# A decoder layer's feed-forward part: three quarters of it dealt out in six eighths, with up products between the two column pairs of each down product

## The chip, the cores and the metric

The kernel runs on one core of a Trainium2 chip. TensorE (PE in the profile, its weight loads PEld) multiplies matrices, VectorE (DVE) and ScalarE (ACT) work on elements, GpSimd (POOL) and SyncE (SP) here mostly start transfers. The metric is the time of one execution in microseconds (us), the median of three runs.

## The reference

A decoder layer for 256 tokens of width 2048, in float32. A first part mixes tokens (attention and a convolution). The second part is a feed-forward layer with a hidden width of 8192:

```
u = rms_norm(h, pre_ff_gain)                      # 256 x 2048
f = square(relu(u @ w_ff1)) @ w_ff2               # 2048 -> 8192 -> 2048
h = h + rms_norm(f, post_ff_gain)
```

The change concerns this part alone. `u @ w_ff1` is called the up product here, the product with `w_ff2` the down product.

## The kernel before

**Numbers.** Each float32 operand of a product is split into a rounded part (hi) and the rest (lo), and a product is three matmuls: hi by hi, hi by lo, lo by hi. A weight chunk of 128 x 2048 (1 MB) is loaded by SP into one of three `raw` buffers (L134), cast to `wh` by ACT (L140) and its rest put into `wl` by DVE (L146). There are three pairs of `wh` and `wl` (`WBUFS`). `take` gives the next prepared chunk, `done` gives one back and prepares the next (`fill`), so that splitting runs up to three chunks ahead in the order of the list `slots`.

**The stream.** The feed-forward part begins with `stream` (L325): `h_sb` is transposed on PE (L332), scaled into the activation tiles `act` (L244, L245), and the first pair of up products is multiplied as the tiles arrive (L259, L262), the second chunk of the pair four tiles (`LAG`) behind the first. Meanwhile `square` (L702) sums up squares for the norm. Behind it the norm's factor is worked out (reduce L734, square root L314, reciprocal L315), laid on a diagonal `dg` (L738) and spread over all partitions by two small matmuls (L739) to `r2b`, which scales every up product.

**Up products.** `ws_pair` (L266) multiplies two weight chunks, one column block each: 16 matmuls of 512 columns (L271: hi and lo of `u` together, by `wh`), then 16 of 256 (L275: `wl`). The result, two blocks of 128 hidden channels, lies in one PSUM tile. `ws_sum` copies one half (L283, ACT), adds the other (L284, DVE, into `z`); then come the product with `r2b` (L893) and the squared ReLU (L896, into `sc`). An even-numbered group of four hidden blocks is laid down by `put_fast` as the seven combinations that a fast unit wants (L765 to L769, `gs`), others by `put_pair` as plain hi and lo (L240, L241, `g`).

**Down products.** The hidden width is worked in four quarters of 16 blocks. In a quarter, all eight up pairs come first, then `fast_pair` for two column pairs m of the output (1024 columns each). A `fast_pair` has four chunks of hidden channels kc, in the order 0, 2, 1, 3. For kc 0 and 1 a *fast unit* does seven products where eight would be plain (Strassen's way), from four weight parts that `fast_part` (L165) makes out of two raw chunks by sums (L162), casts (L156) and subtracts (L157): 42 matmuls (L797, L798, L800). For kc 2 and 3 two plain chunks (one for each 512 columns) do 24 matmuls each (L827 to L829). The products A1 to A7 stand in the order A1, A2, A7, A3, A5, A6, A4. After the second fast unit `combine` puts the products together (one ACT copy L804, four DVE operations L806 to L809) in `ev`; after the last plain chunk of each column block ACT copies the sum to `tmp` (L862). `ev` and `tmp` are added to the total `acc` in SBUF by accumulating transfers that POOL starts (L816, L863). The last `fast_pair` (`closing`) is arranged otherwise, and is the end of the program.

**PSUM.** In this part there are four tiles of two banks, handed out in turn by `new_ps`: an up pair takes one, a `fast_pair` all four (pa to pd); pd is the tile of the last up pair before it, and A3 is its first user.

**What sets the order.** A scheduler orders each engine's instructions by priority. Instructions wrapped in `pin` (`keep_in_program_order`) keep the order in which they are written; those of the stream and of `fast_pair` on PE are, those of `ws_pair` (without `pinned`) are not.

Of the kernel before, what the change touches and what calls it, by code (L numbers as in the profile page):

```python
# [18 lines left out]
P = 128  # L19
S = 256  # L20
# [17 lines left out]
NQ = 4  # L38
# [8 lines left out]
FAST = 2  # L47
FF_ORDER = (0, 2, 1, 3)
# [7 lines left out]
def tile_layer(ctx, tc, x, x_t, pre, vecs, lams, rope_t, subln, b_conv, post_mix, post_ff,  # L56
# [12 lines left out]
    def ff_chunks(q, m):  # L69
        if q == NQ - 1 and m == 1:  # L70
            return [(0, 0), (0, 1), (2, 0), (1, 0), (1, 1), (3, 0), (2, 1), (3, 1)]
        return [(kc, i) for kc in FF_ORDER for i in range(2)]
# [11 lines left out]
    for q in range(NQ):  # L84
        order += [w_f1[q * KT + ct] for ct in range(KT)]
        for m in range(NB // 2):
            order += [w_f2[2 * m + i, q * 4 + kc] for kc, i in ff_chunks(q, m)]
    slots, at = [], 0
    slots += [("chunk", i) for i in range(n_mix)]
    at = n_mix  # L90
    for q in range(NQ):
        slots += [("chunk", at + i) for i in range(KT)]
        at += KT
        for m in range(NB // 2):
            for kc, i in ff_chunks(q, m):
                if kc >= FAST:
                    slots.append(("chunk", at))
                elif i == 0:
                    slots += [(part, at) for part in range(4)]
                at += 1  # L100
# [647 lines left out]
    gsp = ctx.enter_context(tc.tile_pool(name="gsp", bufs=2 * FAST))  # L748
    gpool = ctx.enter_context(tc.tile_pool(name="gpool", bufs=KT // 2 - 2 * FAST))
# [7 lines left out]
    class Mixed(Act):  # L757
        def __init__(self):
            self.tiles = [None] * (KT // 2)
            self.pool, self.name = gpool, "g"  # L760
            self.s = {}
# [11 lines left out]
    def fast_pair(ga, q, m):  # L773
# [4 lines left out]
        closing = q == NQ - 1 and m == 1  # L778
        ev = None if q == 0 else evp.tile([P, NT, 2, 512], F32, name="ev")
        chunks = ff_chunks(q, m)  # L780
        plains = [c for c in chunks if c[0] >= FAST]
# [4 lines left out]
        def part(t, i):  # L786
            return total(t, i) if q == 0 else ev[:, t, i]

        def fast_unit(kc, last):
            for pair in ((A1, A2), (A7, A3), (A5, A6), (A4,)):  # L790
                wh, wl = take()
                for half, a in enumerate(pair):
                    ps = own[a] if a in own else shared[a]
                    for i in range(2):
                        g = ga.s[2 * kc + i]
                        sl = slice(half * 1024 + i * 512, half * 1024 + (i + 1) * 512)
                        pin(nc.tensor.matmul(ps, g[:, 0, a], wh[:, sl], start=(kc == 0 and i == 0), stop=False))  # L797
                        pin(nc.tensor.matmul(ps, g[:, 0, a], wl[:, sl], start=False, stop=False))  # L798
                        ends = last and i == 1 and a in own
# [3 lines left out]
        def combine():  # L803
# [6 lines left out]
            for t in range(NT if q else 0):  # L810
                span = acc[:, t, m * 1024:(m + 1) * 1024]
                half = ev[:, t].rearrange("p i n -> p (i n)")
                if closing:
                    nc.vector.tensor_tensor(span, span, half, op=ALU.add)
                else:
                    nc.gpsimd.dma_start(span, half, accum_op=ALU.add)  # L816
# [21 lines left out]
        for kc, i in chunks:  # L838
            if kc < FAST:
                if i == 0:  # L840
                    fast_unit(kc, kc == FAST - 1)
                    if kc == FAST - 1:
                        combine()
                continue
            if closing and i == 1:
# [5 lines left out]
            if closing and kc == FAST:  # L851
# [5 lines left out]
            if closing:  # L857
# [6 lines left out]
        if closing:  # L864
            plain[0, 1] = new_ps()[:, 0]
            wts = [take(), take()]
            for t in (1, 0):
                for j in range(2):
                    plain_chunk(FAST + j, 1, wts[j], t)
# [17 lines left out]
    for q in range(NQ):  # L887
        ga = Mixed()
        for j in range(KT // 2):
            ps = ws_pair(u2) if q or j else lead_ps  # L890
            z = fin2.tile([P, 2, S], F32, name="z")
            ws_sum(z, ps)
            nc.vector.tensor_tensor(z, z, r2b.unsqueeze(1).to_broadcast([P, 2, S]), op=ALU.mult)  # L893
            sc = fin2.tile([P, 8, P], F32, name="sc", bufs=1)
            gg = sc[:, 0:4].rearrange("p (a t) n -> p a (t n)", a=2)
            nc.vector.scalar_tensor_tensor(gg, z, 0.0, z, op0=ALU.max, op1=ALU.mult)  # L896
            if j < 2 * FAST:
# [86 lines left out]
```

## Time and profile before

| | us |
|---|---|
| median of three runs (1539.47, 1541.21, 1539.69) | 1539.69 |
| the profiled execution's own time | 1541.23 |
| its span | 1539.4 |
| PE busy | 1523.0 (99%) |
| DVE busy | 1274.0 (83%) |
| ACT busy | 786.3 (51%) |
| stream | about 832 to 853 |
| feed-forward part behind it | 853 to 1540 |

The busy times are those of the one profiled execution. A matmul counts as busy from its issue to its end, and neighbours overlap; how many can be issued in a time is read from the starts of neighbouring rows. An idle gap of PE in a part where PE is always busy lengthens the span by itself; idle time of other engines need not.

### The profile page before, as it was taken

Reading aid. Unit: us, or ns where it says so; the run is one execution under the profiler, and the core shown is the slowest. Engines: PE = TensorE matmul, PEld = TensorE weight load, DVE = VectorE, ACT = ScalarE, POOL = GpSimd, SP = SyncE. Lnnn points to the kernel's source line nnn. Section 1 sums busy time; section 2 is a strip of 40 time slices with the busy share of each in tenths; the row PEclk is TensorE's granted clock in tenths of the full one; section 3 lists DMA queues with packets and bytes.
Section 4 is the critical chain, followed back from the end, with each engine's and each line's share of the span. In section 5 each row is a group of like instructions: output and inputs, shape, how many; then the busy total and the mean of one; then the engine's idle time right before and its main releaser. Section 6 shows DMA issues by size and latency. Waiting matters only on the chain.

```text
span 1539.4 us, 19437 instructions
## 1 busy us (share of the span) xinstructions
PE 1523.0 (99%) x7734; PEld 1295.4 (84%) x7734; DVE 1274.0 (83%) x1605; ACT 786.3 (51%) x851; POOL 41.8 (3%) x73
## 2 busy tenths in 40 slices
PE   9999999999999999999999999999999999999997
PEld 7888888888888888888887888888888888888885
DVE  7999999999999997966546888867887778867888
ACT  7444454646554545743435645544455445644454
POOL 0000000000000000000000000000010000110010
PEclk9999999999999999999999999999999999999999
DMA  8655555454445565575554744785478755895673
GB/s 294 225 190 192 192 192 185 171 174 175 174 167 186 192 203 194 181 279 185 189 191 157 267 166 183 226 264 185 170 223 271 228 180 184 246 293 191 233 231 125
DMA packets 51484, 313.66 MB, mean 204 GB/s; under 512 B 5825, under 2 KB 5953, under 8 KB 16705
## 3 DMA queue, kind: packets, MB, share of 16 engines
q1 hardware_dynamic: 43920, 289.61, 52.6%
q0 software_dynamic: 7040, 22.02, 6.1%
q8 instruction: 60, 0.98, 0.2%
q10 hardware_dynamic: 432, 0.79, 0.2%
q14 instruction: 32, 0.25, 0.0%
HBM read 295.62 MB, written 4.19 MB: 195 GB/s over the span
## 4 chain that ended last, share of the span: by engine, by line
PE 92%; DVE 4%; ACT 2%; DMA 1%; issue 1%; SPq 0%; DVEq 0%; ACTq 0%
PE ps L271 29%; PE ps L275 15%; PE ps L292 9%; PE ps L293 9%; PE ps L294 9%; PE ps L828 4%; PE ps L829 4%; PE ps L827 3%; DVE wl L146 2%; ACT wh L140 2%; PE ps L797 2%; PE ps L798 2%; PE ps L800 2%; DMA raw<-in_w_cv_dram 1%; PE po L564 1%
## 5 line engine op out<-in xcount | busy, mean ns | idle before, releaser
L140 ACT CAST wh<-raw 128x2048 fp32r<-128x2048 f32 (+2 forms) x260 | 460.7, 1778 | 495.0 <-PE ps L294 162.6
L146 DVE TENSOR_TENSOR wl<-raw,wh 128x2048 fp32r<-128x2048 f32 (+2 forms) x260 | 551.5, 2125 | 192.5 <-ACT wh L140 188.0
L271 PE MATMUL ps<-act,wh 128*128 128x512 f32 x1984 | 479.1, 392 | 0.3 <-ACT wh L140 0.3
L271 PEld LDWEIGHTS ps<-act,wh 128*128 128x128 f32 x1984 | 364.6, 188 | 70.8 <-ACT wh L140 0.6
L275 PEld LDWEIGHTS ps<-act,wl 128*128 128x128 f32 x1984 | 256.5, 191 | 10.0
L275 PE MATMUL ps<-act,wl 128*128 128x256 f32 x1984 | 264.0, 284 | 0.0
L293 PE MATMUL ps<-wl,act 128*128 128x512 f32 x624 | 243.9, 391 | 0.0
L292 PE MATMUL ps<-wh,act 128*128 128x512 f32 x624 | 243.7, 391 | 0.0
L294 PE MATMUL ps<-wh,act 128*128 128x512 f32 x624 | 243.6, 390 | 0.0
L478 DVE SCALAR_TENSOR_TENSOR y_all<-c,vec,y_all 128x256 f32<-128x256 f32 x480 | 209.9, 478 | 0.0
L294 PEld LDWEIGHTS ps<-wh,act 128*128 128x128 f32 x624 | 117.2, 188 | 24.2
L292 PEld LDWEIGHTS ps<-wh,act 128*128 128x128 f32 x624 | 117.1, 188 | 24.1
L293 PEld LDWEIGHTS ps<-wl,act 128*128 128x128 f32 x624 | 117.2, 188 | 23.9
L156 ACT CAST wh<-raw 128x1024 fp32r<-128x1024 f32 x64 | 65.3, 1050 | 91.1 <-PE ps L829 23.4
L828 PE MATMUL ps<-wl,g 128*128 128x512 f32 x256 | 101.6, 397 | 2.2 <-DVE wl L146 1.2
L829 PE MATMUL ps<-wh,g 128*128 128x512 f32 x256 | 99.7, 390 | 0.0
L827 PE MATMUL ps<-wh,g 128*128 128x512 f32 x256 | 99.7, 390 | 0.0
L798 PE MATMUL ps<-wl,gs 128*128 128x512 f32 x224 | 87.4, 390 | 0.5 <-DVE wl L157 0.5
L797 PE MATMUL ps<-wh,gs 128*128 128x512 f32 x224 | 87.2, 389 | 0.0
L800 PE MATMUL ps<-wh,gs 128*128 128x512 f32 x224 | 87.2, 389 | 0.0
L157 DVE TENSOR_TENSOR wl<-raw,wh 128x1024 fp32r<-128x1024 f32 x64 | 76.3, 1218 | 2.0 <-PE ps L275 1.1
L156 ACT CAST wh<-sum 128x1024 fp32r<-128x1024 f32 x48 | 49.0, 1051 | 37.0 <-PE ps L271 14.3
(200 smaller groups left out, 1253.1 us busy)
## 6 DMA issues: line engine op xcount, KB each, us to landing
raw<-in_w_f_dram SPq DMA_DIRECT2D x124, 1024.0 KB, 5.0
raw<-in_w_q_dram SPq DMA_DIRECT2D x16, 1024.0 KB, 4.9
raw<-in_w_k_dram SPq DMA_DIRECT2D x16, 1024.0 KB, 4.9
raw<-in_w_v_dram SPq DMA_DIRECT2D x16, 1024.0 KB, 4.8
raw<-in_w_ga_dram SPq DMA_DIRECT2D x16, 1024.0 KB, 4.8
raw<-in_w_gc_dram SPq DMA_DIRECT2D x16, 1024.0 KB, 4.9
raw<-in_w_co_dram SPq DMA_DIRECT2D x16, 1024.0 KB, 4.8
raw<-in_w_o_dram SPq DMA_DIRECT2D x16, 1024.0 KB, 4.9
```

Of the source, the lines that this page charges most:

```text
L140: i = nc.scalar.copy(wh[:, a:b], raw[:, a:b])
L146: i = (eng or nc.vector).tensor_sub(wl[:, a:b], raw[:, a:b], wh[:, a:b].bitcast(F32))
L271: a = nc.tensor.matmul(ps[:, j], wh[:, k * P:(k + 1) * P], acts.both(k), start=(k == 0), stop=False)
L275: a = nc.tensor.matmul(ps[:, j, S:], wl[:, k * P:(k + 1) * P], acts.hi(k), start=False, stop=(k == KT - 1))
L292: nc.tensor.matmul(ps, acts.hi(k, a, b), wh[:, sl], start=(k == 0), stop=False)
L293: nc.tensor.matmul(ps, acts.hi(k, a, b), wl[:, sl], start=False, stop=False)
L294: nc.tensor.matmul(ps, acts.lo(k, a, b), wh[:, sl], start=False, stop=(k == KT - 1))
L478: i = nc.vector.scalar_tensor_tensor(y, c[:, j:j + S], vcol(ct, V_DW + j), y, op0=ALU.mult, op1=ALU.add)
L798: pin(nc.tensor.matmul(ps, g[:, 0, a], wl[:, sl], start=False, stop=False))
L827: pin(nc.tensor.matmul(ps, ga.hi(k, a, b), wh[:, sl], start=first, stop=False))
L828: pin(nc.tensor.matmul(ps, ga.hi(k, a, b), wl[:, sl], start=False, stop=False))
L829: pin(nc.tensor.matmul(ps, ga.lo(k, a, b), wh[:, sl], start=False, stop=last))
```

## The change

The first three quarters become six eighths. A list `plan` is written out: four up pairs; then for each eighth e the down product of column pair 0, two up pairs of the next eighth, the down product of column pair 1, two more up pairs; the last quarter stays whole. Each of the six eighths has one fast unit (even kc) and two plain chunks (odd kc) for a column pair. So there are 14 calls of `down` for eight of `fast_pair`, and a combine and two `tmp` sums in each but the last. The weights' list and `slots` follow the plan. The up products are pinned now. Line numbers move by 8 at first and by 9 near the end: L271 becomes L279, L284 L292, L739 L747, L797 L806, L893 L902.

```diff
-FAST = 2
-FF_ORDER = (0, 2, 1, 3)
+GROUPS = ((0, 1), (2, 3), (4, 5), (6, 7), (8, 9), (10, 11), (12, 13, 14, 15))
...
-    def ff_chunks(q, m):
-        if q == NQ - 1 and m == 1:
-            return [(0, 0), (0, 1), (2, 0), (1, 0), (1, 1), (3, 0), (2, 1), (3, 1)]
-        return [(kc, i) for kc in FF_ORDER for i in range(2)]
+    def ff_chunks(e, m):
+        out = [(kc, i) for kc in GROUPS[e] for i in range(2)]
+        if closing(e, m):
+            a, b, c, d = GROUPS[e]
+            out = [(a, 0), (a, 1), (b, 0), (c, 0), (c, 1), (d, 0), (b, 1), (d, 1)]
+        return out
+
+    def is_fast(kc):
+        return kc % 2 == 0
+
+    def closing(e, m):
+        return e == len(GROUPS) - 1 and m == 1
+
+    plan = [("up", j) for j in range(4)]
+    for e in range(len(GROUPS) - 1):
+        ups = [("up", j) for j in range(4 * e + 4, 4 * e + 8)]
+        plan += [("down", (e, 0))] + ups[:2] + [("down", (e, 1))] + ups[2:]
+    e = len(GROUPS) - 1
+    plan += [("up", j) for j in range(4 * e + 4, 4 * e + 8)] + [("down", (e, 0)), ("down", (e, 1))]
 
     order = []
     for ct in range(KT):
@@ -81,23 +94,18 @@
     for w in (w_ga, w_gc, w_co, w_o):
         order += [w[n, kc] for n in range(NB) for kc in range(4)]
     n_mix = len(order)
-    for q in range(NQ):
-        order += [w_f1[q * KT + ct] for ct in range(KT)]
-        for m in range(NB // 2):
-            order += [w_f2[2 * m + i, q * 4 + kc] for kc, i in ff_chunks(q, m)]
-    slots, at = [], 0
-    slots += [("chunk", i) for i in range(n_mix)]
-    at = n_mix
-    for q in range(NQ):
-        slots += [("chunk", at + i) for i in range(KT)]
-        at += KT
-        for m in range(NB // 2):
-            for kc, i in ff_chunks(q, m):
-                if kc >= FAST:
-                    slots.append(("chunk", at))
-                elif i == 0:
-                    slots += [(part, at) for part in range(4)]
-                at += 1
+    slots = [("chunk", i) for i in range(n_mix)]
+    for what, which in plan:
+        if what == "up":
+            slots += [("chunk", len(order) + i) for i in range(2)]
+            order += [w_f1[2 * which + i] for i in range(2)]
+            continue
+        for kc, i in ff_chunks(*which):
+            if not is_fast(kc):
+                slots.append(("chunk", len(order)))
+            elif i == 0:
+                slots += [(part, len(order)) for part in range(4)]
+            order.append(w_f2[2 * which[1] + i, kc])
...
-    def fast_pair(ga, q, m):
+    def down(ga, e, m):
...
-        closing = q == NQ - 1 and m == 1
-        ev = None if q == 0 else evp.tile([P, NT, 2, 512], F32, name="ev")
-        chunks = ff_chunks(q, m)
-        plains = [c for c in chunks if c[0] >= FAST]
+        close = closing(e, m)
+        ev = None if e == 0 else evp.tile([P, NT, 2, 512], F32, name="ev")
+        chunks = ff_chunks(e, m)
+        plains = [c for c in chunks if not is_fast(c[0])]
+        fasts = [kc for kc, i in chunks if is_fast(kc) and i == 0]
...
-            return total(t, i) if q == 0 else ev[:, t, i]
-
-        def fast_unit(kc, last):
+            return total(t, i) if e == 0 else ev[:, t, i]
+
+        def fast_unit(kc):
...
-                        pin(nc.tensor.matmul(ps, g[:, 0, a], wh[:, sl], start=(kc == 0 and i == 0), stop=False))
+                        pin(nc.tensor.matmul(ps, g[:, 0, a], wh[:, sl], start=(kc == fasts[0] and i == 0), stop=False))
                         pin(nc.tensor.matmul(ps, g[:, 0, a], wl[:, sl], start=False, stop=False))
-                        ends = last and i == 1 and a in own
+                        ends = kc == fasts[-1] and i == 1 and a in own
                         pin(nc.tensor.matmul(ps, g[:, 1, a], wh[:, sl], start=False, stop=ends))
...
-    for q in range(NQ):
-        ga = Mixed()
-        for j in range(KT // 2):
-            ps = ws_pair(u2) if q or j else lead_ps
-            z = fin2.tile([P, 2, S], F32, name="z")
-            ws_sum(z, ps)
-            nc.vector.tensor_tensor(z, z, r2b.unsqueeze(1).to_broadcast([P, 2, S]), op=ALU.mult)
-            sc = fin2.tile([P, 8, P], F32, name="sc", bufs=1)
-            gg = sc[:, 0:4].rearrange("p (a t) n -> p a (t n)", a=2)
-            nc.vector.scalar_tensor_tensor(gg, z, 0.0, z, op0=ALU.max, op1=ALU.mult)
-            if j < 2 * FAST:
-                ga.put_fast(j, sc)
-            else:
-                ga.put_pair(j, gg)
-        if q == NQ - 1:
+    ga = Mixed()
+
+    def up(j):
+        ps = ws_pair(u2, pinned=True) if j else lead_ps
+        z = fin2.tile([P, 2, S], F32, name="z")
+        ws_sum(z, ps)
+        nc.vector.tensor_tensor(z, z, r2b.unsqueeze(1).to_broadcast([P, 2, S]), op=ALU.mult)
+        sc = fin2.tile([P, 8, P], F32, name="sc", bufs=1)
+        gg = sc[:, 0:4].rearrange("p (a t) n -> p a (t n)", a=2)
+        nc.vector.scalar_tensor_tensor(gg, z, 0.0, z, op0=ALU.max, op1=ALU.mult)
+        if is_fast(j // 2):
+            ga.put_fast(j, sc)
+        else:
+            ga.put_pair(j, gg)
+
+    for what, which in plan:
+        if what == "up":
+            up(which)
+            continue
+        e, m = which
+        if (e, m) == (len(GROUPS) - 1, 0):
...
-        for m in range(NB // 2):
-            fast_pair(ga, q, m)
+        down(ga, e, m)
```

Three places show how the order moves. First TensorE at the end of the stream: `dg` is the norm's factor on a diagonal, L259/L262 and L267/L270 are the stream's own matmuls. Before:

```order
L259 MATMUL ps<-act,wh 128x512
L262 MATMUL ps<-act,wl 128x256
L271 MATMUL ps<-act,wh 128x512
L275 MATMUL ps<-act,wl 128x256 x10
L739 MATMUL aux<-dg,ones 128x128 x2
L275 MATMUL ps<-act,wl 128x256 x6
L271 MATMUL ps<-act,wh 128x512 x16
```
After:

```order
L267 MATMUL ps<-act,wh 128x512
L270 MATMUL ps<-act,wl 128x256
L747 MATMUL aux<-dg,ones 128x128 x2
L279 MATMUL ps<-act,wh 128x512 x16
L283 MATMUL ps<-act,wl 128x256 x16
```

The 16 wide matmuls of the next up pair's first chunk (L271) no longer stand between the stream's; they stand behind the broadcast of `dg`, which has moved from between the narrow ones to directly behind the stream.

Second, VectorE behind the stream, from the reduction of the sums of squares (`hss`) to the first whole weight chunk. Before:

```order
L734 TENSOR_REDUCE r_6953<-hss 128x2
L315 RECIPROCAL r_6953<-r_6953 128x2
L738 TENSOR_SCALAR dg<-ident,r_6953 128x128 x2
L146 TENSOR_TENSOR wl<-raw,wh 128x512 x4
L146 TENSOR_TENSOR wl<-raw,wh 128x2048
```
After:

```order
L742 TENSOR_REDUCE r_6953<-hss 128x2
L154 TENSOR_TENSOR wl<-raw,wh 128x512 x4
L323 RECIPROCAL r_6953<-r_6953 128x2
L746 TENSOR_SCALAR dg<-ident,r_6953 128x128 x2
L154 TENSOR_TENSOR wl<-raw,wh 128x2048
```

The four subtracts of the third weight chunk's quarters have moved ahead of the reciprocal and of `dg`.

Third, VectorE ahead of a fast unit, from the first sum of its two raw chunks to the add into `z` of the last up pair (L284, now L292); `g`, `sc` belong to the up pairs, `sum` and the 128x1024 `wl` to the fast unit. Before, second quarter, first column pair:

```order
L162 TENSOR_TENSOR sum<-raw 128x1024
L162 TENSOR_TENSOR raw<-raw 128x2x512
L157 TENSOR_TENSOR wl<-raw,wh 128x1024 x2
L162 TENSOR_TENSOR sum<-raw 128x1024
L284 TENSOR_TENSOR z<-z,ps 128x512
L162 TENSOR_TENSOR sum<-sum,raw 128x1024
L893 TENSOR_TENSOR z<-z,r2b 128x512
L157 TENSOR_TENSOR wl<-raw,wh 128x1024 x2
L896 SCALAR_TENSOR_TENSOR sc<-z 128x512
L157 TENSOR_TENSOR wl<-sum,wh 128x1024 x2
L241 TENSOR_TENSOR g<-sc,g 128x2x256
L284 TENSOR_TENSOR z<-z,ps 128x512
```
After, second eighth, second column pair (two subtracts of 128x1024, the fast unit's first part, stand directly ahead of it):

```order
L170 TENSOR_TENSOR sum<-raw 128x1024
L292 TENSOR_TENSOR z<-z,ps 128x512
L170 TENSOR_TENSOR raw<-raw 128x2x512
L902 TENSOR_TENSOR z<-z,r2b 128x512
L165 TENSOR_TENSOR wl<-raw,wh 128x1024
L170 TENSOR_TENSOR sum<-raw 128x1024
L905 SCALAR_TENSOR_TENSOR sc<-z 128x512
L165 TENSOR_TENSOR wl<-raw,wh 128x1024
L170 TENSOR_TENSOR sum<-sum,raw 128x1024
L773 TENSOR_TENSOR sc<-sc 128x256
L165 TENSOR_TENSOR wl<-sum,wh 128x1024 x2
L292 TENSOR_TENSOR z<-z,ps 128x512
```

The two sums from raw stood ahead of the first part's subtracts (L157) and now stand behind them, mixed with the work on `z`; the add into `z` of the last up pair is still behind the third part's subtracts.

## Rows read from the trace of the kernel before

**Rows 1.** Page, part 1: engine, busy us (share of span), instructions

```profile
PE 1523.0 (99%) x7734; PEld 1295.4 (84%) x7734; DVE 1274.0 (83%) x1605; ACT 786.3 (51%) x851; POOL 41.8 (3%) x73
```

**Rows 2.** Windows: bounds and length, busy us of each engine, granted clock, DMA, GB/s

```profile
830.00:833.00 3.00, 1.48 (x8) 0.65 (x7) 2.45 (x7) 1.46 (x4) 0.00 (x0) 1.00 0.72 300
835.00:838.30 3.30, 3.30 (x13) 2.73 (x13) 2.30 (x6) 2.25 (x7) 0.00 (x0) 0.51 0.00 0
832.30:850.60 18.30, 17.65 (x94) 14.82 (x94) 13.31 (x27) 14.10 (x36) 1.06 (x2) 0.91 0.32 118
853.33:1530.00 676.67, 673.94 (x3413) 571.03 (x3411) 547.28 (x498) 348.86 (x321) 35.97 (x43) 1.00 0.64 214
```

**Rows 3.** Timeline of PE: start, us, line, operation, tiles, count

```profile
1094.63 3.82 PE L271 MATMUL ps<-act,wh 128*128 128x512 f32 x16
...
1100.20 0.40 PE L797 MATMUL ps<-wh,gs 128*128 128x512 f32 x1
...
1104.31 0.39 PE L797 MATMUL ps<-wh,gs 128*128 128x512 f32 x1
...
1109.74 0.39 PE L827 MATMUL ps<-wh,g 128*128 128x512 f32 x1
1110.20 0.50 PE L828 MATMUL ps<-wl,g 128*128 128x512 f32 x1
1110.54 0.39 PE L829 MATMUL ps<-wh,g 128*128 128x512 f32 x1
```

**Rows 4.** Waits of PE: waiting line, releaser, us in all, times, longest

```profile
PEld ps L828 <- DVE wl L146: 8.9, 16, 1.6
```

**Rows 5.** Timelines of DVE and ACT beside the same fast unit

```profile
1100.47 2.36 DVE L157 TENSOR_TENSOR wl<-sum,wh 128x1024 fp32r<-128x1024 f32 x2 [2.43 <-PE ps L275]
1102.74 0.69 DVE L241 TENSOR_TENSOR g<-sc,g 128x512 fp32r<-128x512 f32 x1
1103.35 0.68 DVE L284 TENSOR_TENSOR z<-z,ps 128x512 f32<-128x512 f32 x1
...
1103.20 1.05 ACT L156 CAST wh<-sum 128x1024 fp32r<-128x1024 f32 x1 [1.66 <-PE ps L800]
...
1107.85 2.29 DVE L146 TENSOR_TENSOR wl<-raw,wh 128x2048 fp32r<-128x2048 f32 x1 [1.36 <-ACT wh L140]
```

**Rows 6.** Timeline of PE: a long fast unit, its first instruction and the one behind it

```profile
1162.52 0.39 PE L797 MATMUL ps<-wh,gs 128*128 128x512 f32 x1
...
1172.23 0.39 PE L827 MATMUL ps<-wh,g 128*128 128x512 f32 x1
```

**Rows 7.** Groups by form, 870 to 1540: busy us, mean ns, idle before

```profile
L162 DVE TENSOR_TENSOR sum<-raw 128x1024 f32<-128x1024 f32 x32 | 39.0, 1220 | 7.0 <-DMA raw<-in_w_f_dram 6.8
...
L806 DVE TENSOR_TENSOR z<-ev,ps 128x512 f32<-128x512 f32 x6 | 4.1, 679 | 0.0
```

**Rows 8.** Timeline of PE: the end of the stream

```profile
853.09 0.40 PE L271 MATMUL ps<-act,wh 128*128 128x512 f32 x1
853.33 1.35 PE L275 MATMUL ps<-act,wl 128*128 128x256 f32 x10
...
855.68 0.64 PE L271 MATMUL ps<-act,wh 128*128 128x512 f32 x2
```

**Rows 9.** Timelines of ACT and DVE behind the stream: root, dg, casts

```profile
850.66 0.30 ACT L314 ACTIVATE r<-r,epsn 128x2 f32<-128x2 f32 x1 [0.23 <-DVE r L734]
...
851.19 0.48 DVE L738 TENSOR_SCALAR dg<-ident,r 128x128 f32<-128x128 f32 x2
...
851.40 2.19 ACT L140 CAST wh<-raw 128x512 fp32r<-128x512 f32 x4 [0.44 <-PE ps L259]
```

**Rows 10.** Raw loads: the page's median to landing, and one load behind a burst

```profile
raw<-in_w_f_dram SPq DMA_DIRECT2D x124, 1024.0 KB, 5.0
...
L134 SPq DMA_DIRECT2D raw<-in_w_f_dram x1: 327/327/327, 1188.0 to 1188.0; - x1
...
DMA to landing us min/median/max: 9.2/9.2/9.2
```

More of the change, by code (lines that the diff above doesn't have):

```diff
@@ L36 @@
 NEG_INF = -1e30
-NQ = 4
 WBUFS = 3
@@ L747, in tile_layer @@
     sump = ctx.enter_context(tc.tile_pool(name="sump", bufs=3))
-    gsp = ctx.enter_context(tc.tile_pool(name="gsp", bufs=2 * FAST))
-    gpool = ctx.enter_context(tc.tile_pool(name="gpool", bufs=KT // 2 - 2 * FAST))
+    gsp = ctx.enter_context(tc.tile_pool(name="gsp", bufs=4))
+    gpool = ctx.enter_context(tc.tile_pool(name="gpool", bufs=4))
     evp = ctx.enter_context(tc.tile_pool(name="evp", bufs=1))
@@ L758, in __init__ @@
         def __init__(self):
-            self.tiles = [None] * (KT // 2)
+            self.tiles = [None] * (DFF // S)
             self.pool, self.name = gpool, "g"
@@ L809, in combine @@
             nc.vector.tensor_tensor(part(0, 1), own[A5], part(0, 0), op=ALU.subtract)
-            for t in range(NT if q else 0):
+            for t in range(NT if e else 0):
                 span = acc[:, t, m * 1024:(m + 1) * 1024]
                 half = ev[:, t].rearrange("p i n -> p (i n)")
-                if closing:
+                if close:
                     nc.vector.tensor_tensor(span, span, half, op=ALU.add)
@@ L838, in fast_pair @@
         for kc, i in chunks:
-            if kc < FAST:
+            if is_fast(kc):
                 if i == 0:
-                    fast_unit(kc, kc == FAST - 1)
-                    if kc == FAST - 1:
+                    fast_unit(kc)
+                    if kc == fasts[-1]:
                         combine()
                 continue
-            if closing and i == 1:
+            if close and i == 1:
                 continue
@@ L850, in fast_pair @@
             done()
-            if closing and kc == FAST:
+            if close and (kc, i) == plains[0]:
                 for n in range(2):
@@ L856, in fast_pair @@
                 continue
-            if closing:
+            if close:
                 first_half()
@@ L863, in fast_pair @@
                     nc.gpsimd.dma_start(total(t, i), tmp[:, t], accum_op=ALU.add)
-        if closing:
+        if close:
             plain[0, 1] = new_ps()[:, 0]
@@ L868, in fast_pair @@
                 for j in range(2):
-                    plain_chunk(FAST + j, 1, wts[j], t)
+                    plain_chunk(plains[-2 + j][0], 1, wts[j], t)
                 with tc.high_priority(offset=CHAIN):
```

## The prediction

> **What bounds the kernel now.** I read the page's busy shares first, then a table of windows, then TensorE's own sequence. PE is busy 99% of the span, DVE 83%, ACT 51% [rows 1]. The windows show that the feed-forward part (853.33 to 1530.00) is fuller still: PE 673.94 of 676.67 us, DVE 547.28, ACT 348.86, at full clock [rows 2]. So there the time is the number of TensorE instructions times their issue spacing, and whatever PE waits comes on top. In a steady stretch matmuls of 512 columns start 0.227 us apart: the 18 from 1100.20 to 1104.31 take 4.11 us, and the fast unit (42 matmuls) 9.54, from 1100.20 to 1109.74 [rows 3]. A weight chunk of the up products (16 of 512 columns, 16 of 256) takes 1100.20 - 1094.63 = 5.57. A plain chunk is 24 matmuls, 5.44.
>
> Only two kinds of PE wait recur. The first plain chunk behind a fast unit loses 0.35 us at its second instruction: 1109.74 to 1110.54 holds two spacings (0.45) and takes 0.80 [rows 3]. The waits put it down to DVE's wl, 16 times [rows 4]. The reason can be read on DVE: that chunk's subtract (2.29 us, at 1107.85) waits 1.36 for its cast [rows 5], the cast for the wh slot that the first part of the fast unit's four frees; cast and subtract take longer than the matmuls still ahead of them. The second kind is a late fast part: the unit begun at 1162.52 took 9.71, to 1172.23, 0.2 more than its 42 spacings [rows 6]. On that point the Trainium skill ("Perfetto Trace Analysis", section "Identifying the Most-Contended Engine") says matmul busy time is a poor measure of headroom and the busy share of weight loads a better one. Its measure gives 571.03 of 676.67, 84%, some headroom in which a small wait could be caught up, and the waits below would cost nothing; the constant 0.227 leaves none, and I go by the measurement.
>
> **The change part by part.**
> The matmuls of the feed-forward part are the same in kind and number: sixteen fast units, sixteen pairs of plain chunks, 64 up chunks. On TensorE that is 0. There are fourteen downs for eight, so six more combines: 24 DVE instructions of 0.679 [rows 7], 16.3 us, and 30 more ACT copies; DVE goes to (547.28 + 16.3) / 676.67 = 83% of the part. The 36 added accumulating transfers occupy POOL's queue, which waits for nothing urgent. What hides all this is that PE is the bound, so averaged it costs 0; what counts is where DVE comes late.
>
> *Start of the part.* The up products are now pinned to program order. Before, the scheduler put the 16 wide matmuls of the next pair's first chunk between the transposes and matmuls of the stream (the last at 853.09), so behind it only the 16 narrow ones remained; they end at 855.68 [rows 8]. Now the 16 wide ones stand behind the stream, and L747, the broadcast of dg, stands in front of them on PE's queue. Whoever is queued behind L747 waits for it: all of PE. Two lists changed with it: on DVE the four subtracts of 128x512 precede the reciprocal, and on ACT the four casts (2.19 us) precede the square root. Before, the root came at 850.66 and dg was begun at 851.19, ahead of the casts at 851.40 [rows 9].
> The sum, in before's time axis: the stream loses 16 x 0.227 = 3.63 us of PE work, but the other chain in it, ACT's, was busy 14.10 of 18.30 us [rows 2], so that its 4.2 us of idle time are the most that can go. Sixteen hand-overs from PE to ACT and back keep part of these: I put the most at 3.0, the least at 1.1, and take 2.0, near the middle. The stream then ends at 853.3 - 2.0 = 851.3. The casts wait for the last wide matmul on the stream's first chunk, four pairs of 0.35 before the end, so they run 850.0 to 852.2; root to first L747 is 0.8 (0.53 to dg, a dg of 0.24), so 853.0; the first L279 at 853.3; the chunk ends 5.57 later at 858.9. Against 855.68 that is **+3.2 us**. By the two ends of the shrinking it is +2.2 or +4.1.
>
> *The wait in front of A3.* The fourth product group of a fast unit in order of execution (A3 in the code) begins 18 matmuls in, at 1104.31, and writes the PSUM tile that the last up pair used, so it waits for DVE's add into z. Before, this add ran from 1103.35 for 0.68 [rows 5], to 1104.03: 0.28 early. Counted from the unit's start the add may begin at +3.4. Now it depends on what DVE has to do from the moment that the unit's two raw chunks are there and first needed, 8.6 us ahead of the unit (two chunks of 5.57 minus the two subtracts, 1.14 apart by 1100.47 to 1102.74 [rows 5], begun 0.27 after a slot is freed). For the downs (e,1) with e from 1 the list shown above then runs: sum, z add (0.6), sum of two raws, the cast of it (1.05 [rows 5], the z product inside it), subtract, sum, 0.6, subtract, sum, 0.33, two subtracts. That is eight DVE steps of 1.14 (the sums cost as much, 1.22 each with their overlap [rows 7]), 1.53 of short ones and the cast: 9.12 + 1.53 + 1.05 = 11.7, so the z add starts at +3.1 to +3.25, and there is nothing to spare. For the downs (e,0) with e from 2 a subtract of g (0.61) stands in it instead of the 0.33 one: +3.4 to +3.5, a loss of 0.1. For the first three and the last, DVE does the two sums before the subtracts, as before, and nothing is lost.
> So the loss is set by when the raw chunks land. A load lands after 5.0 us in the median, but the one issued at 1188.0 took 9.2 [rows 10], behind the accumulating transfers of the down that ended at 1172.23 + 11.3 = 1183.5 [rows 6]. It stands where a fast unit's second raw will now stand, four up chunks (22.3 us) ahead of 1205.8: it lands at 1197.2, exactly the 8.6 ahead. Before, a quarter's first fast unit came 16 up chunks (89 us) behind such a burst; now eleven come four behind one. With raws on time the nine places lose 4 x 0.1, 0.4 in all; with each 0.35 late, 5 x 0.23 + 4 x 0.48 = 3.1. I take the middle, **+1.7**, since the one load seen there is exactly on the edge. Ends: 0 and 5 (each late by 0.55).
>
> *Small.* The slip in the unit at 1162.52, the fourth of four downs in a row, I read as a raw load late behind a burst; that place no longer exists: -0.2. The 16 losses of 0.35 stay, because slots and casts per fast unit are the same: 0.
>
> The sum is 3.2 + 1.7 - 0.2 = **+4.7 us**. The profiled execution took 1541.23 (span 1539.4 and 1.8 around it), so 1545.9 in its terms; it was 1.54 above the median of 1539.69, against which the forecast is **1544.4**. About 0.2%, 3.1 us, can be told from no change; the bound lies at 1542.8.
>
> **The rivals.**
> 1. *Only the start costs* (A3's wait is covered, as DVE gains time from the thinner stretches): for it speaks that my walk misses the edge by a tenth; against it the 9.2 us landing. 3.2 - 0.2: 1542.7.
> 2. *The stream shrinks fully.* If PE's order alone set the stream (it was busy 17.65 of 18.30 us there [rows 2]), all 3.63 come off: 5.2 - 3.6 = +1.6, less 0.2, A3 covered: 1541.1.
> 3. *The other side: the 0.35 losses go.* One mechanism: with up products spread out, DVE and ACT have earlier free time, the first plain chunk's split is done before the fast unit ends, 16 x 0.35 = 5.6 gained, against 3.2 lost: 1537.3. It decides once the split can start 0.35 earlier. Against it: cast and subtract wait for a slot that the same PE instruction frees, not for a busy engine; for it, nothing in the rows.
> 4. *Raws come late for all eleven fast units behind a burst*, a microsecond each instead of a few tenths: 1539.7 + 3.0 + 11 = 1554, at half of it 1549.
> 5. *DVE becomes the bound* in the stretches of one down and two ups: all 16.3 us show, 1556. Against it 83%.
> 6. *The clock.* Before, PE did 1.48 us of work in 830 to 833 and the granted clock then stood at 0.51 over 835.00 to 838.30, 1.2 GHz of 2.4 [rows 2]. The new gap in front of L747 is about 1.7 us. If the clock falls again, 3.3 us at half speed cost about 1.6: 1546. The Trainium skill ("TensorE: Matmul & The Clock Gate", section "What's actually happening") says that the throttled state is the default and activity releases it; the trace agrees with 0.51 behind the idle stretch, and no row shows what a gap of 1.7 does.
>
> **How the numbers follow.** Forecast (both losses, with the clock in its margin) 0.52; rival 1 0.15, rival 2 0.10, rival 3 0.07, rival 4 0.13, rival 5 0.03. The range 1541.0 to 1549.5 holds the forecast with its ends (2.2 + 0.4 to 4.1 + 3.1 + 1.6), rivals 1 and 2, and the mild half of 4; out are 3, 5 and the rest of 4, under 0.2. Faster: rival 3, 0.06. Within 0.2%: half of rival 1, nearly all of 2 and the low end of the forecast, 0.28. Slower: 0.66.
>
> **What would show it.** At the start: PE idle 1.5 to 2 us until L747, ended by DVE's dg, and the first L279 near 853. Fast units of 9.7 to 10.0 instead of 9.54 at five to nine of the sixteen, with the wait at the first L806 behind 18 matmuls, ended by DVE's z (L292). The wait of plain chunks for wl still 16 times. Wrong would be: L747 without a wait, no L806 waiting for z, or waits of fast units at their first instructions for raw data.

## The result and the profile after

The changed kernel is slower. Its median is 1549.03 us (1546.82 to 1550.83, four runs) beside 1540.45 (four runs) for the kernel before; the ratio is 1.0055, 95% interval [1.0043, 1.0067]. A second series, against other runs of the kernel before, gave 1547.55 beside 1540.18: 1.0045 [1.0031, 1.0059]. So the change costs 7.4 to 8.6 us; 4.7 was forecast. The profiled execution took 1547.95 with a span of 1546.2, 6.8 more than the span before, and nearly all of these 6.8 can be found in the trace.

First the page: part 1 (busy time of each engine), and the row of part 6 for the weight loads (count, size, median time from issue to landing).

```profile
PE 1524.5 (99%) x7734; PEld 1295.2 (84%) x7734; DVE 1281.0 (83%) x1629; ACT 799.0 (52%) x881; POOL 72.4 (5%) x109
...
raw<-in_w_f_dram SPq DMA_DIRECT2D x124, 1024.0 KB, 6.9
```

PE has the same 7734 instructions and, to 1.5 us, the same busy time as in [rows 1]; DVE has its 24 more. The shares say nothing of the loss. The row of the loads does: a weight chunk lands 6.9 us after its issue in the median, 5.0 before [rows 10].

The waits of PE tell where the time is (the waiting line, what it waited for, us in all, times, longest).

```profile
PE ps L806 <- DVE z L292: 2.9, 3, 1.3
PE aux L747 <- DVE dg L746: 1.9, 1, 1.9
...
PE ps L807 <- DVE wl L165: 0.5, 1, 0.5
```

L747 waits for dg, and three times the first matmul behind 18 of a fast unit (L806) waits for z. Neither row stood there before. The wait of plain chunks is still there on the weight loads' queue:

```profile
PEld ps L837 <- DVE wl L154: 9.2, 16, 1.6
```

**The start.** PE's timeline behind the stream (start, us, line, count, idle time before it and what ended it):

```profile
848.65 0.28 PE L270 MATMUL ps<-act,wl 128*128 128x256 f32 x1
850.81 0.68 PE L747 MATMUL aux<-dg,ones 128*128 128x128 f32 x4 [1.88 <-DVE dg L746]
851.25 5.53 PE L279 MATMUL ps<-act,wh 128*128 128x512 f32 x16
856.62 2.06 PE L283 MATMUL ps<-act,wl 128*128 128x256 f32 x16
858.51 3.82 PE L279 MATMUL ps<-act,wh 128*128 128x512 f32 x16
```

Beside it ACT and DVE, where the root (L322) and dg (L746) stand behind four casts and four subtracts:

```profile
847.11 2.18 ACT L148 CAST wh<-raw 128x512 fp32r<-128x512 f32 x4 [0.27 <-PE ps L267]
849.20 0.29 ACT L322 ACTIVATE r<-r,epsn 128x2 f32<-128x2 f32 x1
...
847.77 2.50 DVE L154 TENSOR_TENSOR wl<-raw,wh 128x512 fp32r<-128x512 f32 x4 [0.73 <-ACT wh L148]
850.19 0.16 DVE L323 RECIPROCAL r<-r 128x2 f32<-128x2 f32 x1
850.38 0.48 DVE L746 TENSOR_SCALAR dg<-ident,r 128x128 f32<-128x128 f32 x2
```

The chunk ends at 858.51, where before it ended at 855.68 [rows 8]. To that 2.83 comes that the part ahead of the stream, which the change doesn't touch, ended earlier here: its last matmul in this trace and in the trace before (one fence each):

```profile
829.33 0.39 PE L302 MATMUL aux<-wh,act 128*128 128x512 f32 x1
```

```profile
830.04 0.39 PE L294 MATMUL aux<-wh,act 128*128 128x512 f32 x1
```

Counted from there the start loses 3.5 us. The 16 wide matmuls at 851.25 took 5.37 us instead of the 3.66 of the next 16, because the clock fell. The granted clock is the third column from the end of these windows:

```profile
834.00:838.00 4.00, 3.77 (x21) 2.85 (x21) 3.82 (x9) 3.58 (x11) 0.00 (x0) 1.00 0.00 0
851.00:855.00 4.00, 4.00 (x14) 3.21 (x14) 3.58 (x3) 1.03 (x3) 0.00 (x0) 0.57 1.00 406
```

Before, the low stretch lay early in the stream, 0.51 over 835.00 to 838.30 [rows 2], and the clock was full behind it. Here it is full early and falls behind the wait for dg.

**The long fast units.** Reading PE's timeline from one unit to the next gives the length of all sixteen fast units. Twelve take 9.52 to 9.57 us, the usual length before; the closing one 10.33, about as before (10.31). Three more are long: 929.39 to 940.32 (10.93), 974.11 to 985.30 (11.19) and 1320.02 to 1330.41 (10.39). Together with 0.30 in a plain pair they cost 4.2 us. A down is named here by its eighth e and its column pair m. The three are the downs (0,1), (1,0) and (5,0). In the first, PE:

```profile
929.39 0.40 PE L806 MATMUL ps<-wh,gs 128*128 128x512 f32 x1
...
934.75 0.50 PE L806 MATMUL ps<-wh,gs 128*128 128x512 f32 x1 [1.09 <-DVE z L292]
...
940.32 0.39 PE L836 MATMUL ps<-wh,g 128*128 128x512 f32 x1
```

and DVE in the same unit, ten microseconds earlier and beside it:

```profile
920.19 1.23 DVE L170 TENSOR_TENSOR sum<-raw 128x1024 f32<-128x1024 f32 x1 [4.94 <-DMA raw<-in_w_f_dram]
921.33 1.22 DVE L165 TENSOR_TENSOR wl<-raw,wh 128x1024 fp32r<-128x1024 f32 x1
...
934.01 0.68 DVE L292 TENSOR_TENSOR z<-z,ps 128x512 f32<-128x512 f32 x1
```

DVE stood idle for 4.94 us with a sum at the head of its list, whose second raw chunk had not landed. The subtract behind it in the list needed no more than the first raw chunk and its cast. DVE carried this lateness through the list to the add into z, 4.62 us behind the unit's start, where +3.4 would have done. The view of that load (issued at 911.6; who waited for it; time to landing):

```profile
L142 SPq DMA_DIRECT2D raw<-in_w_f_dram x1: 328/328/328, 911.6 to 911.6; - x1
...
  DVE sum L170: 4.9, 1
...
DMA to landing us min/median/max: 8.5/8.5/8.5
```

The down (1,0) is the same case: its load took 8.6 us, and its sum waited 5.10.

The unit at 1018.76 (down (1,1)) is the counterpart. Its load issued at 1001.0 took longer still, 9.7 us, and the unit took 9.55. There the list has the two subtracts first, and they fill the wait:

```profile
1008.32 2.36 DVE L165 TENSOR_TENSOR wl<-raw,wh 128x1024 fp32r<-128x1024 f32 x2 [2.56 <-ACT wh L164]
1010.67 1.23 DVE L170 TENSOR_TENSOR sum<-raw 128x1024 f32<-128x1024 f32 x1
...
1021.90 0.68 DVE L292 TENSOR_TENSOR z<-z,ps 128x512 f32<-128x512 f32 x1
```

The third long unit, (5,0), has the subtracts first as well, and is long for another reason: here the *first* raw chunk was late. Its load, issued at 1297.9, took 11.2 us; the cast (L164) waited for it, the subtracts for the cast:

```profile
1309.22 2.00 ACT L164 CAST wh<-raw 128x1024 fp32r<-128x1024 f32 x2 [4.28 <-DMA raw<-in_w_f_dram]
...
1310.30 2.36 DVE L165 TENSOR_TENSOR wl<-raw,wh 128x1024 fp32r<-128x1024 f32 x2 [3.03 <-ACT wh L164]
...
1324.06 0.68 DVE L292 TENSOR_TENSOR z<-z,ps 128x512 f32<-128x512 f32 x1
```

One figure tells the long units from the usual ones. From its first instruction on a unit's raw chunks to the add into z, DVE's list takes 13.5 to 13.9 us in eleven of the twelve units of the eighths (15.0 in the first, where it began 11.9 us ahead). It began 9.2, 9.05 and 9.7 us ahead of the three long units, and 10.4 to 10.9 ahead of the other eight. A list with a sum at its head begins when the second raw chunk has landed, one with a subtract when a slot is free and the first has landed and is cast.

The account of the span: start 3.5, three long units 1.4 + 1.6 + 0.8, a plain pair 0.3; against it 0.7 from the part ahead of the stream and 0.2 where the long unit of [rows 6] was: 6.7 of 6.8 us.

### The profile page after: what moved, and what is told of

Read it like the earlier page. It is cut to its first block, busy times and chain, and to the rows that moved or that the text cites. A ratio compares the mean times of both kernels' runs of the same rounds, so it can differ in the third digit from the quotient of the medians.

```text
span 1546.2 us, 19603 instructions
## 1 busy us (share of the span) xinstructions
PE 1524.5 (99%) x7734; PEld 1295.2 (84%) x7734; DVE 1281.0 (83%) x1629; ACT 799.0 (52%) x881; POOL 72.4 (5%) x109
## 3 DMA queue, kind: packets, MB, share of 16 engines
q0 software_dynamic: 12224, 34.61, 10.4%
## 4 chain that ended last, share of the span: by engine, by line
PE 87%; DVE 6%; DMA 3%; ACT 2%; issue 1%; SPq 0%; DVEq 0%; ACTq 0%
PE ps L279 27%; PE ps L283 14%; PE ps L302 9%; PE ps L301 9%; PE ps L300 9%; PE ps L837 4%; PE ps L838 3%; PE ps L836 3%; DVE wl L154 3%; ACT wh L148 2%; PE ps L806 2%; DMA raw<-in_w_f_dram 2%; PE ps L809 2%; PE ps L807 2%; DVE wl L165 1%; DMA raw<-in_w_cv_dram 1%
## 5 line engine op out<-in xcount | busy, mean ns | idle before, releaser
L279 PE MATMUL ps<-act,wh 128*128 128x512 f32 x1984 | 477.5, 392 | 0.2 <-ACT wh L148 0.2
L279 PEld LDWEIGHTS ps<-act,wh 128*128 128x128 f32 x1984 | 366.2, 189 | 71.8 <-ACT wh L148 0.6
L164 ACT CAST wh<-raw 128x1024 fp32r<-128x1024 f32 x64 | 65.3, 1050 | 97.4 <-PE ps L279 33.5
L165 DVE TENSOR_TENSOR wl<-raw,wh 128x1024 fp32r<-128x1024 f32 x64 | 76.6, 1220 | 20.0 <-PE ps L283 11.6
L806 PE MATMUL ps<-wh,gs 128*128 128x512 f32 x224 | 87.7, 391 | 2.9 <-DVE z L292 2.9
L164 ACT CAST wh<-sum 128x1024 fp32r<-128x1024 f32 x48 | 48.8, 1049 | 59.0 <-PE ps L279 30.8
```

The source lines that it names most:

```text
L279: a = nc.tensor.matmul(ps[:, j], wh[:, k * P:(k + 1) * P], acts.both(k), start=(k == 0), stop=False)
```

## The experiments

Two theories stood against each other for the units. A: a late load costs where DVE's list has the sum ahead of the subtracts. B: late loads cost wherever they are. For the start the question was whether the pin and the place of dg are the cause. Medians are compared with runs of the kernel before on the same chip.

**1. The kernel before, pinned** (`before_pinned`)

```diff
-            ps = ws_pair(u2) if q or j else lead_ps
+            ps = ws_pair(u2, pinned=True) if q or j else lead_ps
```

> The kernel before with its up products pinned to program order and nothing else changed; on VectorE and ScalarE the four subtracts and casts then stand ahead of the reciprocal, the root and dg, as in the changed kernel. Theory: the pinning costs what the start of the feed-forward part lost in the changed kernel's trace (first chunk behind the stream ends 2.8 us later): 1540.4 + 2.8 = 1543.2, with a wait of about 1.9 us in front of the broadcast of dg and a granted clock near one half behind it. Rival: the start loss belongs to something else in the new plan (the raw loads' order, the earlier first fast unit): then 1540.4, no wait.

Measured: 1544.23 beside 1540.63, 1.0023 [1.0014, 1.0033]. The wait is the same to the hundredth:

```profile
851.84 0.68 PE L739 MATMUL aux<-dg,ones 128*128 128x128 f32 x4 [1.88 <-DVE dg L738]
852.28 3.92 PE L271 MATMUL ps<-act,wh 128*128 128x512 f32 x16
856.03 2.08 PE L275 MATMUL ps<-act,wl 128*128 128x256 f32 x16
```

The first fast unit began 2.3 us later than before (930.31 for 928.05), and counted from the end of the part ahead of the stream (829.67 for 830.04) 2.6 us. So the start loss belongs to the pin with its two lists. The expected clock behind the wait was a miss: it was full there (the 16 wide ones end after 3.75), and 0.58 over 834 to 838, in the stream. A unit of the third quarter that took 10.08 and a plain pair of 11.53 add 0.8. The stream, from the end of the part ahead of it to its last matmul, took 20.3 us where it took 23.3 before. The rival, that the rest of the new plan is at fault, falls for the start.

**2. The first part's subtracts pinned ahead of the sums** (`after_wlfirst`)

```diff
-            split_sum(wt, 0, w11)
-            split_sum(wt, 1, w21)
+            split_sum(wt, 0, w11, True)
+            split_sum(wt, 1, w21, True)
...
+            i = nc.vector.tensor_tensor(sums[name], a, b, op=ALU.add)
+            if name == "t1":
+                pin(i)
```

> The changed kernel, with VectorE's two subtracts of a fast unit's first part pinned ahead of the first sum of its two raw chunks in all sixteen units. Theory A (list and late load together): the fast units at 929 and 974 were long because VectorE waited 4.9 and 5.1 us for a raw chunk at a sum with the subtracts of the first part queued behind it; with the subtracts ahead both units take 9.55 instead of 10.93 and 11.19, 3 us less or more: about 1545.5. Theory B (late loads alone): a raw chunk that lands 8 to 9 us after its issue delays a fast unit whatever the list: 1549, the same total loss of about 4 us in fast units, perhaps elsewhere.

Measured: 1558.24, 1.0112 [1.0097, 1.0128]. Neither theory gave this. The pin did more than was meant: the scheduler moved all sums of a unit behind the work on z as well, so that units took 9.81 and 11.17 in turn, with waits of another kind:

```profile
PE ps L812 <- DVE wl L165: 8.3, 7, 1.3
PE ps L842 <- DVE wl L154: 6.3, 8, 1.8
```

It does not decide between A and B. It shows that the order of the lists on DVE and ACT (ACT's changed along with DVE's) can be worth 9 us here, with every instruction and PE's order the same.

**3. Without the accumulating transfers of the eighths** (`after_noacc`; their sums are left out of the total)

```diff
-                else:
+                elif e == len(GROUPS) - 1:
                     nc.gpsimd.dma_start(span, half, accum_op=ALU.add)
...
+                    if e == len(GROUPS) - 1:
+                        nc.gpsimd.dma_start(total(t, i), tmp[:, t], accum_op=ALU.add)
```

> The changed kernel without the accumulating transfers of the six eighths (their sums are not added to the total; the copies and combines stay). Theories A and B alike: raw chunks land in about 5 us, no fast unit over 9.6, and only the start loss of 2.8 is left: 1543.3. Rival C: the long fast units come from VectorE's added work and order, not from late loads: still 10.9 and 11.2 at the same two places, 1548 to 1549.

Measured: 1546.30, 1.0032 [1.0020, 1.0045]; the profiled execution 1544.96. The page's row of the loads:

```profile
raw<-in_w_f_dram SPq DMA_DIRECT2D x124, 1024.0 KB, 4.9
```

So it is these transfers that slow the weight loads. The units at the two places are 9.90 and 9.55 now instead of 10.93 and 11.19, and rival C falls for them. But six of all the units take 9.86 to 10.24: without the transfers the scheduler wrote another list, with a subtract of `gs` (1.08 us) between the third part's subtracts and the add into z, and the add comes too late by 0.3. In this list all twelve units of the eighths have the sums first. The median is 3 us above what was expected, of which these six make 2.3.

**4. dg earlier** (`after_dg`)

```diff
-    nc.vector.tensor_reduce(r2, hss, axis=AX.X, op=ALU.add)
-    rsqrt(r2, r2, epsn, 1.0 / D)
     pr2 = aux_ps()[:, 0:S]
+    with tc.high_priority(offset=CHAIN):
+        nc.vector.tensor_reduce(r2, hss, axis=AX.X, op=ALU.add)
+        rsqrt(r2, r2, epsn, 1.0 / D)
+        for t in range(NT):
+            nc.vector.tensor_scalar(dg[:, t], ident, r2[:, t:t + 1], None, op0=ALU.mult)
     for t in range(NT):
-        nc.vector.tensor_scalar(dg[:, t], ident, r2[:, t:t + 1], None, op0=ALU.mult)
```

> The changed kernel with a higher priority for the norm's reduction, root, reciprocal and dg: the root now stands behind one of the four casts instead of behind four, dg behind two subtracts instead of four. Theory: PE's wait in front of the broadcast of dg falls from 1.9 to about 0.8 us: 1548.0; and if the shorter gap keeps the clock up, the 1.7 us of half-clock behind it go as well: 1546.3. Rival: the wait is set by the end of the stream's squares, not by the casts: 1549, wait unchanged.

Measured: 1546.23, 1.0033 [1.0022, 1.0044].

```profile
849.46 0.68 PE L749 MATMUL aux<-dg,ones 128*128 128x128 f32 x4 [0.58 <-DVE dg L747]
849.89 3.91 PE L279 MATMUL ps<-act,wh 128*128 128x512 f32 x16
```

The wait fell from 1.88 to 0.58, the clock behind it is full, and the first fast unit starts at 883.38 instead of 886.35. Counted from the end of the part ahead of the stream (829.08), the start loss is 0.8 instead of 3.5. The median is 2.8 below that of the changed kernel's first series, as the theory with the clock had it, but only 1.3 below that of its second (1547.55). That the shorter gap kept the clock up is not shown: in experiment 9 the clock is full behind a wait of 1.85, and the loss is 2.6. Between that trace and this one, both with the half-clock stretch early (0.57 over 832 to 836 here), the loss falls by 1.8: 1.3 at the wait, 0.5 in the stream. The other 0.9 of the first trace's 3.5 came from where its half-clock stretch fell. The same three units are long (10.73, 11.27, 10.65).

**5. A few transfers less** (`after_quiet`; the plain sums of the first eighth and of down (4,1) are left out of the total)

```diff
+                    if not (e == 0 or (e, m) == (4, 1)):
+                        nc.gpsimd.dma_start(total(t, i), tmp[:, t], accum_op=ALU.add)
```

> The changed kernel without twelve of its accumulating transfers: the plain sums of the first eighth (both column pairs) and those of the fifth eighth's second column pair aren't added to the total. VectorE's list still has the sums of raw ahead of the first part's subtracts in the second and third down, and now also in the eleventh (e = 5, m = 0). Theory A (list and late load together): the loads ahead of the second and third down land in about 5 us instead of 8.5, so these units take 9.9 (the z add behind a subtract of gs, as in the run without transfers) and 9.55 instead of 10.93 and 11.19, and the eleventh 9.55 to 9.9 instead of 10.39: about 3.5 us less, 1545.5. Theory B' (the sums' place in the list alone is the cause): the second and third down stay near 11, and the eleventh, which has the sums first now, gets longer: 1550.

Measured: 1546.17, 1.0041 [1.0029, 1.0054]. The two units take 9.90 and 9.54, with the sums still first in the list, and the load ahead of the second of them (8.6 us in the changed kernel, issued at 956.4) takes 4.9:

```profile
972.22 0.40 PE L806 MATMUL ps<-wh,gs 128*128 128x512 f32 x1
...
981.76 0.39 PE L836 MATMUL ps<-wh,g 128*128 128x512 f32 x1
```

```profile
L142 SPq DMA_DIRECT2D raw<-in_w_f_dram x1: 328/328/328, 954.4 to 954.4; - x1
...
DMA to landing us min/median/max: 4.9/4.9/4.9
```

So a list with the sums first costs nothing here with loads on time, and experiment 3 says the same: B' falls. What speaks for A and against B is the changed kernel's first trace: eight units with the subtracts first kept their 9.55 though the load of their second chunk took 8.3 to 9.7 us. No run set the two orders against each other with all else equal, since experiment 2 missed that. Three things missed. The unit of down (5,0) still took 10.49: the list there changed to sums first, and the other transfers ahead of it (`ev`) had stayed. And (3,0) took 9.65 and (3,1) 10.11, where the changed kernel's first trace had 9.55, both with the subtracts first. In (3,1) the second raw chunk came so late that the two subtracts no longer covered the wait for it:

```profile
1176.91 2.36 DVE L165 TENSOR_TENSOR wl<-raw,wh 128x1024 fp32r<-128x1024 f32 x2 [1.62 <-PE ps L283]
1180.36 1.23 DVE L170 TENSOR_TENSOR sum<-raw 128x1024 f32<-128x1024 f32 x1 [1.08 <-DMA raw<-in_w_f_dram]
```

So theory A holds within limits: the subtracts at the head hide up to 2.3 us of a late second chunk, and nothing of a late first one.

**6. Only the second up pair not pinned** (`after_loose1`)

```diff
-        ps = ws_pair(u2, pinned=True) if j else lead_ps
+        ps = ws_pair(u2, pinned=j > 1) if j else lead_ps
```

> The changed kernel with the second up pair (the first behind the stream) not pinned; all else pinned as it is. The 16 wide matmuls then stand in the stream again and dg stands ahead of the four subtracts, as before the change. Theory: the start loss goes, 2.8 less, the long fast units stay about as they are (4 us): 1546.0. Rival: what the pin costs is the clock's fall alone, and that comes as often without it: 1549.

Measured: 1551.19, 1.0064 [1.0052, 1.0077]. The start is as hoped (first fast unit at 882.77, 3.6 earlier than in the changed kernel), and the loss comes back at once: that unit takes 12.21.

```profile
884.00 0.50 PE L806 MATMUL ps<-wh,gs 128*128 128x512 f32 x1 [0.37 <-ACT gs L776]
886.46 0.50 PE L809 MATMUL ps<-wh,gs 128*128 128x512 f32 x1 [1.73 <-DVE gs L777]
```

Its `gs` are not ready: in the new plan only four up pairs precede the first fast unit, where eight did, and in the loose order their work on DVE falls behind. So the pin cannot simply be dropped for this plan. Five more units of this trace are long, 11.05, 11.51, 10.01, 10.47 and 10.56, about 2 us more in all than the three of the changed kernel; with the 2.7 of the first unit that is more than the start gave. The median lies 2.1 above this execution (1549.05), and why is not shown.

**7. The kernel before, first plain chunk split in halves** (`before_halves`)

```diff
+            if slots[state["next"] - 2][0] == 3:
+                w = CHUNK // 2
-            for j in range(pieces):
+            for j in range(CHUNK // w):
                 split_hi(chunk, j * w, (j + 1) * w)
```

> The kernel before with the first plain chunk behind a fast unit cast and subtracted in two halves of 1024 columns instead of at once; nothing else changed. Theory (the wait of 0.35 us at the second instruction of a plain chunk is the time that cast 1.91 and subtract 2.29 take beyond the 18 matmuls ahead of them): with halves the first wl is there 1.05 + 1.14 + a little behind the free slot, inside the 4.08 us, and 16 waits of 0.35 go: 1540.6 - 5.6 = 1535.0. Rival: the slot frees later than thought or the wait moves to the second half: less than 2 us gained.

Measured: 1534.85 beside 1540.41, 0.9966 [0.9954, 0.9979]: 5.6 us faster.

```profile
1108.35 0.39 PE L829 MATMUL ps<-wh,g 128*128 128x512 f32 x1
1108.58 0.39 PE L830 MATMUL ps<-wl,g 128*128 128x512 f32 x1
1108.81 0.39 PE L831 MATMUL ps<-wh,g 128*128 128x512 f32 x1
```

The second instruction follows after 0.23 instead of 0.46 [rows 3], and every whole pair of plain chunks ahead of the closing ones takes 10.88, which is 48 spacings. It is the fastest of all versions run.

**8. Both cures on the changed kernel** (`after_dg_halves`: the edits of 4 and 7 together)

```diff
+    with tc.high_priority(offset=CHAIN):
+        nc.vector.tensor_reduce(r2, hss, axis=AX.X, op=ALU.add)
...
+            if slots[state["next"] - 2][0] == 3:
+                w = CHUNK // 2
```

> The changed kernel with the higher priority for dg and with the first plain chunk behind each fast unit split in halves. The waits of 0.35 go as in the kernel before with halves (5.6 us) from the 1546.2 of the version with the higher priority: 1540.6, if the long fast units stay; VectorE's list has the first part's subtracts ahead or beside the sums in more of the downs now, which would take up to 3 us more off: 1537.6.

Measured: 1539.87, 0.9996 [0.9987, 1.0005]. The 16 losses go here too; the units of (0,1) and (1,0) are still long (10.82 and 11.20), all others but the closing one (10.84) 9.52 to 9.57. (5,0) is among these; its first raw chunk landed 12.9 us ahead of it here, 10.9 in the changed kernel. So the changed plan comes back to the time of the kernel before with cures that would make the old plan faster.

**9. The changed kernel again** (`after_again`: no edit)

> The changed kernel once more, for a second trace. Theory A (list and late load): the same units, those of the second and third down, are long again by 1.2 to 1.7 us, since their list has the sums first and their loads come behind the same transfers; the eleventh, whose list has the subtracts first, is long or not as its loads land, 9.5 to 10.7. The start's loss is 2 to 3 us, wherever the clock falls. Median 1549 within 1. Rival (chance): other units are long, and the second and third down are not.

Measured: 1547.55. The units of (0,1) and (1,0) took 10.79 and 10.77, that of (5,0) 10.29, and (1,1) 10.27 and (3,0) 9.82 this time; the start lost 2.6 from the end of the part ahead of the stream (830.42), with full clock behind the wait (1.85 us) and 0.60 over 834 to 838.

```profile
852.55 0.68 PE L747 MATMUL aux<-dg,ones 128*128 128x128 f32 x4 [1.85 <-DVE dg L746]
```

So the two places with the sums first stay long. (5,0) stays long too, with the subtracts first: it took 10.3 to 10.7 in both traces of the changed kernel and in those of experiments 4 and 6, and each time the load of its first raw chunk took 11.1 or 11.2 us. Between the two traces of the changed kernel only (1,1) and (3,0) come and go; their first raw chunks landed 11.1 and 11.4 us ahead of them here, and 11.6 and 11.9 in the first trace. The median lies 1.5 under the expected one.

## Why the prediction was right

It was right in its sign and in where the time goes, and too small: 4.7 us for 7.4 to 8.6. The first series' median of 1549.03 lies only 0.5 under the upper end of its range.

*Start, +3.2 forecast, 3.5 and 2.6 in two traces.* The mechanism is shown: experiment 1 brings it into the old kernel, experiment 4 takes most of it out of the new. That the sum came so near is in part luck, since its terms were mis-sized both ways. The stream was put 2.0 shorter; with the half-clock stretch in it, as before, it was 3.0 shorter (20.3 us in the second trace and in experiment 1, for 23.3). In the first trace it was 3.7 shorter (829.33 to 848.9), because the clock stayed up in it; the clock's fall, which stood in rival 6 as a risk, came behind the gap instead and cost 1.7. Behind a wait of 1.8 to 1.9 it fell in one of six traces. From the root to the first L747 0.8 was put, and it took 1.6 (849.20 to 850.81): the reciprocal and dg stand behind the four subtracts, which the prediction names and its sum leaves out. Against that the casts began about 0.5 earlier, counted from the stream's end, than was put. Where the half-clock stretch of some 3 us falls differs between two executions of the changed kernel. That the spread of the medians comes from it is argued, not shown.

*A3's wait, +1.7 forecast, 4.2 and 4.6 with the plain pair.* The wait is the one described (L806 for z behind 18 matmuls) and its cause is late raw chunks, as said. The step that failed is "For the first three and the last, DVE does the two sums before the subtracts, as before, and nothing is lost." Two of these were the longest units of all. I had walked the list as if the sums could always start, and looked only at how much stands between the sums and the add. What counts is what stands at the head while a load is late: a sum that needs both chunks holds up 2.3 us of subtracts that need one. Of the nine places where I looked for the loss, one in the first trace and three in the second showed it, and there the late chunk was the first of the two, where I had reckoned with the second. In the undisturbed ones the add began 2.6 to 3.1 us behind the unit's start, so the 0.1 that four of them were to lose with loads on time did not come. The load at 9.2 us [rows 10] was the right row; what it meant for each place was read wrongly. The term's arithmetic is also a little off: a lateness of 0.35 less the slack of 0.15 to 0.3 (+3.1 to +3.25 against +3.4) is 0.05 to 0.2, not 0.23, which makes the term up to 0.4 smaller.

*Rival 3* named a real 5.6 us, but not something the change reaches: the wait stayed at 16 times, and went only in experiment 7, when the chunk was split.

*The other rivals.* Rivals 1 and 2 take A3's wait as covered, and it cost over 4 us; that the stream shrank by 3.7 in the first trace (0.7 of it by the clock), as much as rival 2 has it, did not help, because L747 waited for dg. Rival 4 gives the measured 1549 "at half of it" (half of its 11 us makes 1548.2), but not by its mechanism: three to five of eleven units were late, not all. Rival 5 falls with the eight units of the eighths that ran at their usual 9.55 behind the added combines.

*Small.* The -0.2 came. The 24 added DVE instructions and 36 transfers cost nothing as work, as the 9.55 of the undisturbed units shows; the transfers cost by the loads that they slow.

## What to carry to other kernels

On an engine that takes its list in order, ask of every instruction at the head: which transfer does it wait for, and what behind it could have run? A list that is good with loads on time can be bad with loads late: the sums at the head cost nothing at 4.9 us and 1.2 to 1.7 at 8.2 to 8.7. Ask it of both loads, since a subtract at the head helps only when its own chunk has landed. When a change adds transfers, look at the time to landing of the others before counting busy shares. And a small wait that recurs with the same size is worth splitting the piece that it waits for: sixteen of them gave more than the whole change cost in any one of its terms.

## What was not expected of the hardware

A 1 MB weight load of this part lands in 4.9 us in the median without the accumulating transfers of the eighths and in 6.9 with them, 11.6 at the most (6.7 and 12.1 in the second trace). By what path the transfers slow the loads is not shown. A half-clock stretch of TensorE of some 3 us appeared between 832 and 855 us in all traces of this study but that of experiment 8, at different places: 0.60 over 834 to 838 in the kernel before and in the second trace of the changed kernel, 0.57 over 851 to 855 in its first, the only trace that has it behind the stream. And the part ahead of the stream, with the same instructions in every version, ended anywhere from 829.08 to 830.65, so that a difference of under 1.5 us between two spans says nothing by itself.
